# A softmax over 16,384 rows: the first tile loaded in two pieces, and fewer rows scaled on ScalarE

## The chip, the cores and the metric

The kernel runs on one core of one Trainium2 chip. The metric is device time in microseconds (us). The profile's span is about 1.8 us shorter than the time of the same run (160.7 against 162.45 in the kernel before). All runs quoted here were in the same state, called fast, with a granted clock of 1.0 (the share of its full speed that the profile records). The kernel before takes 162.57 us in the median of three runs (162.41 to 162.81). In the batches that follow its median moved between 162.58 and 162.72, so every ratio is taken against the runs of the kernel before in the same session, on the same chip; where two times of different sessions are set side by side, the text says so.

## The reference

```python
def reference(x):                       # x: 16 x 1024 x 512, float32
    x_scaled = x / 0.5
    x_max = np.max(x_scaled, axis=-1, keepdims=True)
    exp_x = np.exp(x_scaled - x_max)
    return exp_x / np.sum(exp_x, axis=-1, keepdims=True)
```

The input is 33.55 MB and so is the output. Each must cross the DMA once: 67.1 MB that no rearrangement of the arithmetic can avoid (the page of the kernel before has 33.55 MB read and 33.55 MB written).

## The kernel before

The 16,384 rows are cut into eight tiles. A tile has 128 partitions with 16 rows of 512 numbers on each (4 MB). The kernel keeps six tiles on the chip at once, so load 6 waits until store 0 has landed, and load 7 waits for store 1 (in the trace the stores land at 69.6 and 89.0 us, and the loads are issued at 69.7 and 89.1). Each tile is worked in blocks of rows: VectorE finds the negated maximum and doubles it (`shift`), ScalarE takes the exponentials row by row and sums them, VectorE inverts the sums, and then VectorE and ScalarE share the scaling.

```python
G = 16                                            # rows per partition and tile
WHOLE = [(0, G)]
LOADS = [[(0, 1), (1, 4), (4, G)]] + [WHOLE] * 7
BLOCKS = [[(0, 4), (4, 8), (8, G)]] + [WHOLE] * 6 + [[(0, 8), (8, G)]]
STORES = [WHOLE] * 8
# ... (cut)
def scale_vector(i):
    c, lo, hi = blocks[i]
    b = hi - lo
    k = b - b // 4                                # VectorE's rows of the block
    # ... reciprocal of the sums (cut)
    rows = chunks[c][:, lo : lo + k, :]
    nc.vector.tensor_mul(
        rows, rows, recips[i][:, 0:k].unsqueeze(2).broadcast_to((P, k, D)))

def scale_scalar(i):                              # ScalarE's rows of the block
    c, lo, hi = blocks[i]
    b = hi - lo
    for g in range(b - b // 4, b):
        row = chunks[c][:, lo + g, :]
        nc.scalar.activation(out=row, in_=row, func=COPY, scale=recips[i][:, g : g + 1])
# ... (cut)
shift(0); shift(1); exponentials(0)
for i in range(n):                                # n = 11 blocks
    if i + 1 < n: exponentials(i + 1)
    scale_vector(i)
    scale_scalar(i)
    if i + 2 < n: shift(i + 2)
    store(i)                                      # issued by ScalarE when the tile is complete
```

Of the kernel before, what the change touches and what calls it, by code (L numbers as in the profile page):

```python
# [1 line left out]

# [4 lines left out]


@with_exitstack
def kernel(  # L10
    ctx: ExitStack,
    tc: tile.TileContext,
    x: bass.AP,
    out: bass.AP,
):
    nc = tc.nc
    fp32 = mybir.dt.float32
    P = nc.NUM_PARTITIONS
    AX = mybir.AxisListType.X
    EXP = mybir.ActivationFunctionType.Exp  # L20
    COPY = mybir.ActivationFunctionType.Copy
    MAX = mybir.AluOpType.max

    D = x.shape[-1]
    xf = x.flatten_outer_dims()
    of = out.flatten_outer_dims()
    N = xf.shape[0]




    G = 16
    C = N // (P * G)
    assert C * P * G == N
    xr = xf.rearrange("(c p g) d -> c p g d", p=P, g=G)
    outr = of.rearrange("(c p g) d -> c p g d", p=P, g=G)
    WHOLE = [(0, G)]
    LOADS = [[(0, 1), (1, 4), (4, G)]] + [WHOLE] * 7
    BLOCKS = [[(0, 4), (4, 8), (8, G)]] + [WHOLE] * 6 + [[(0, 8), (8, G)]]
    STORES = [WHOLE] * 8  # L40
    BMAX = 16
    BUFS = 6

    data = ctx.enter_context(tc.tile_pool(name="data", bufs=BUFS))
    stats = ctx.enter_context(tc.tile_pool(name="stats", bufs=6))

    ctx.enter_context(tc.manual_schedule())


    warm = stats.tile([P, 1], fp32, name="warm", bufs=1)  # L50
    nc.vector.memset(warm, 0.0)  # L51
    nc.scalar.activation(out=warm, in_=warm, func=EXP)  # L52

    chunks = {}
    blocks = [(c, lo, hi) for c in range(C) for lo, hi in BLOCKS[c]]
    n = len(blocks)
    biases, sums, recips = {}, {}, {}

    def load(c):
        if c < BUFS:  # L60
            chunks[c] = data.tile([P, G, D], fp32, name="xt")
        else:
            chunks[c] = chunks[c - BUFS]
        xt = chunks[c]
        for lo, hi in LOADS[c]:
            nc.sync.dma_start(out=xt[:, lo:hi, :], in_=xr[c][:, lo:hi, :])  # L66

    def shift(i):
        c, lo, hi = blocks[i]
        if c not in chunks:  # L70
            load(c)
        b = hi - lo
        negmax = stats.tile([P, BMAX], fp32, name="negmax")
        nc.vector.tensor_reduce(  # L74
            negmax[:, 0:b], chunks[c][:, lo:hi, :], axis=AX, op=MAX, negate=True
        )
        biases[i] = stats.tile([P, BMAX], fp32, name="bias")
        nc.vector.tensor_scalar_mul(biases[i][:, 0:b], negmax[:, 0:b], 2.0)  # L78

    def exponentials(i):  # L80
        c, lo, hi = blocks[i]
        sums[i] = stats.tile([P, BMAX], fp32, name="sums")
        for g in range(hi - lo):
            row = chunks[c][:, lo + g, :]
            nc.scalar.activation(  # L85
                out=row,
                in_=row,
                func=EXP,
                bias=biases[i][:, g : g + 1],
                scale=2.0,  # L90
                accum_out=sums[i][:, g : g + 1],
            )


    def scale_vector(i):
        c, lo, hi = blocks[i]
        b = hi - lo
        k = b - b // 4
        recips[i] = stats.tile([P, BMAX], fp32, name="recip")
        nc.vector.reciprocal(recips[i][:, 0:b], sums[i][:, 0:b])  # L100
        rows = chunks[c][:, lo : lo + k, :]
        nc.vector.tensor_mul(  # L102
            rows, rows, recips[i][:, 0:k].unsqueeze(2).broadcast_to((P, k, D))
        )

    def scale_scalar(i):
        c, lo, hi = blocks[i]
        b = hi - lo
        for g in range(b - b // 4, b):
            row = chunks[c][:, lo + g, :]  # L110
            nc.scalar.activation(  # L111
                out=row, in_=row, func=COPY, scale=recips[i][:, g : g + 1]
            )

    def store(i):
        c, _, end = blocks[i]
        for lo, hi in STORES[c]:
            if hi == end:
                nc.scalar.dma_start(  # L119
                    out=outr[c][:, lo:hi, :], in_=chunks[c][:, lo:hi, :]  # L120
                )

    shift(0)
    shift(1)
    exponentials(0)
    for i in range(n):
        if i + 1 < n:
            exponentials(i + 1)
        scale_vector(i)
        scale_scalar(i)  # L130
        if i + 2 < n:
            shift(i + 2)
        store(i)


# [1 line left out]
_INS = ['x']  # L137
_OUTS = [((16, 1024, 512), 'float32')]


# [23 lines left out]
```

## Time and profile before

| | before |
|---|---|
| time | 162.57 us |
| VectorE (DVE) busy | 125.6 us, 78% of the span |
| ScalarE (ACT) busy | 112.5 us, 70% |
| DMA | 9 tenths or more in all slices but the first and the last |
| last store issued, and landed | 140.3 us, 159.6 us |

The first lines of the page: busy time by engine, then the span in 40 equal slices (each digit is the busy share in tenths), and what the DMA moved in each.

```profile
span 160.7 us, 421 instructions
## 1 busy us (share of the span) xinstructions
DVE 125.6 (78%) x45; ACT 112.5 (70%) x290; POOL 0.2 (0%) x4
## 2 busy tenths in 40 slices
DVE  0507999999999999999999999999799994800000
ACT  3071759089989989995999599959998969600000
...
DMA  5999999999999999999999999999999999999993
```

VectorE and ScalarE stop some 20 us before the end, and the DMA does not. That points to the DMA as the bound; e4 below tests it. How hard the DMA works is in the view by stretches of time (start and end of the stretch in us, its length, busy us of each engine, then the clock, the DMA's share and GB/s):

```profile
5.00:45.00 40.00, 34.23 (x17) 25.24 (x68) 0.00 (x0) 1.00 1.01 434
45.00:90.00 45.00, 44.83 (x11) 41.71 (x109) 0.00 (x0) 1.00 1.01 426
90.00:130.00 40.00, 38.69 (x13) 35.88 (x92) 0.00 (x0) 1.00 1.00 433
...
140.00:156.00 16.00, 0.24 (x1) 0.00 (x0) 0.00 (x0) 1.00 1.00 432
```

The rate is the same 426 to 434 GB/s whether the DMA only loads (first line), loads and stores, or only stores (last line). The trace's record of single packets says the same thing more sharply: 96% of the 32 KB packets hold their DMA engine for 1.213 us, and 16 engines x 32,768 bytes / 1.213 us = 432 GB/s.

The costs that the change touches are in the groups of instructions (line of the code, engine, operation, shapes, count, then total us, mean ns of one, and idle time before them):

```profile
L74 DVE TENSOR_REDUCE negmax<-xt 128x16 f32<-128x8192 f32 x6 | 52.1, 8678 | 0.0
L102 DVE TENSOR_TENSOR xt<-xt,recip 128x6144 f32<-128x6144 f32 x6 | 39.3, 6558 | 0.2
L111 ACT ACTIVATE xt<-xt,recip 128x512 f32<-128x512 f32 x32 | 20.5, 706 | 0.0
L74 DVE TENSOR_REDUCE negmax<-xt 128x8 f32<-128x4096 f32 x3 | 13.2, 4414 | 1.1 <-DMA xt<-in_x_dram 1.1
L102 DVE TENSOR_TENSOR xt<-xt,recip 128x3072 f32<-128x3072 f32 x3 | 10.1, 3358 | 0.1
```

A multiply of 12 rows takes 6558 ns and one of 6 rows 3358 ns, so a row costs (6558 - 3358) / 6 = 533 ns on VectorE in this multiply. And the end of the timeline (start us, duration us, engine, line, operation; in brackets the idle time before it and what ended it):

```profile
136.51 2.55 ACT L111 ACTIVATE xt<-xt,recip 128x512 f32<-128x512 f32 x4
136.65 0.20 DVE L100 RECIPROCAL recip<-sums 128x8 f32<-128x8 f32 x1 [2.32 <-ACT xt L85]
136.88 3.36 DVE L102 TENSOR_TENSOR xt<-xt,recip 128x3072 f32<-128x3072 f32 x1
140.32 0.34 ACTq L119 DMA_DIRECT2D out_dram<-xt  x1
```

The last line is the last store's issue. It lands only 19.2 us later, because nearly the whole of the store before is still ahead of it: in the packet records that one's packets run from 138.93 to 149.54 us, and the last store's own begin at 148.61. That queue is the slack of the arithmetic.

### The profile page before, as it was taken

The page shows a single profiled execution, that of the slowest core. Times are in us where ns is not written, and L with a number is a line of the kernel's source. Part 1 is how long each engine was busy: PE and PEld are TensorE (multiplying, and loading weights), DVE is VectorE, ACT ScalarE, POOL GpSimd, SP SyncE. Part 2 cuts the span into 40 slices and gives each one's busy share as a digit, 9 for nine tenths or more (in the row PEclk, how much of TensorE's full clock was granted, in tenths as well). Part 3 has the DMA queues.
Part 4 walks back from the last instruction along what each step waited for, and adds up shares of the span by engine and source line. Part 5 has one row for each costly group of instructions (what it writes and reads, how often), then busy time and mean ns, then how long its engine had stood idle before and what let it go on. Part 6 is the DMA issues. An engine that isn't in the chain of part 4 may idle for free.

```text
span 160.7 us, 421 instructions
## 1 busy us (share of the span) xinstructions
DVE 125.6 (78%) x45; ACT 112.5 (70%) x290; POOL 0.2 (0%) x4
## 2 busy tenths in 40 slices
DVE  0507999999999999999999999999799994800000
ACT  3071759089989989995999599959998969600000
POOL 0000000000000000000000000000000000000000
DMA  5999999999999999999999999999999999999993
GB/s 169 477 398 465 449 392 465 449 392 443 465 392 392 400 392 498 416 392 473 441 394 457 449 400 441 465 400 432 473 400 416 481 400 416 489 400 408 498 400 139
DMA packets 2595, 67.13 MB, mean 418 GB/s; under 512 B 289, under 2 KB 289, under 8 KB 545
## 3 DMA queue, kind: packets, MB, share of 16 engines
q1 hardware_dynamic: 1440, 33.56, 49.3%
q10 hardware_dynamic: 1152, 33.55, 48.4%
q14 instruction: 3, 0.02, 0.0%
HBM read 33.55 MB, written 33.55 MB: 418 GB/s over the span
## 4 chain that ended last, share of the span: by engine, by line
DMA 41%; DVE 24%; ACT 19%; issue 1%; SPq 1%; ACTq 0%
DMA xt<-in_x_dram 23%; DMA out_dram<-xt 18%; ACT xt L85 17%; DVE negmax L74 15%; DVE xt L102 8%; ACT xt L111 2%; DVE bias L78 1%; SPq L66 1%; DVE recip L100 0%; ACTq L119 0%; ACTq L85 0%
## 5 line engine op out<-in xcount | busy, mean ns | idle before, releaser
L85 ACT ACTIVATE xt<-xt,bias 128x512 f32<-128x512 f32 x128 | 90.4, 707 | 25.8 <-DVE bias L78 24.8
L74 DVE TENSOR_REDUCE negmax<-xt 128x16 f32<-128x8192 f32 (+2 forms) x11 | 69.9, 6353 | 10.7 <-DMA xt<-in_x_dram 10.7
L102 DVE TENSOR_TENSOR xt<-xt,recip 128x6144 f32<-128x6144 f32 (+2 forms) x11 | 52.9, 4813 | 0.4
L85 ACT ACTIVATION_READ_ACCUMULATOR xt<-xt,bias 128x1 f32 x128 | 23.9, 187 | 0.0
L111 ACT ACTIVATE xt<-xt,recip 128x512 f32<-128x512 f32 x32 | 20.5, 706 | 0.0
L100 DVE RECIPROCAL recip<-sums 128x16 f32<-128x16 f32 (+2 forms) x11 | 2.4, 218 | 2.3 <-ACT xt L85 2.3
L78 DVE TENSOR_SCALAR bias<-negmax 128x16 f32<-128x16 f32 (+2 forms) x11 | 1.9, 173 | 0.4
L52 ACT ACT_TABLE_LOAD x1 | 1.3, 1283 | 0.7 <-PEq L148 0.7
L51 DVE MEMSET warm<- 128x1 f32 x1 | 0.1, 59 | 0.8 <-PEq L148 0.8
L52 ACT ACTIVATE warm<-warm 128x1 f32<-128x1 f32 x1 | 0.2, 203 | 0.0
L148 POOL MEMSET const-bfloat16-1.0<- 128x1 bf16 x1 | 0.1, 102 | 0.0
L148 POOL MEMSET const-uint8-127<- 128x1 uint8 x1 | 0.1, 102 | 0.0
L148 POOL MEMSET const-float32-0.0<- 128x1 f32 x1 | 0.1, 99 | 0.2 <-issue 0.2
L148 POOL MEMSET const-float32-1.0<- 128x1 f32 x1 | 0.1, 99 | 0.0
## 6 DMA issues: line engine op xcount, KB each, us to landing
out_dram<-xt ACTq DMA_DIRECT2D x8, 4096.0 KB, 24.8
xt<-in_x_dram SPq DMA_DIRECT2D x7, 4096.0 KB, 29.8
xt<-in_x_dram SPq DMA_DIRECT2D x1, 3072.0 KB, 11.3
xt<-in_x_dram SPq DMA_DIRECT2D x1, 768.0 KB, 4.5
xt<-in_x_dram SPq DMA_DIRECT2D x1, 256.0 KB, 2.8
```

The costliest lines, as they stand in the source:

```text
L51: nc.vector.memset(warm, 0.0)
L52: nc.scalar.activation(out=warm, in_=warm, func=EXP)
L66: nc.sync.dma_start(out=xt[:, lo:hi, :], in_=xr[c][:, lo:hi, :])
L74: nc.vector.tensor_reduce(negmax[:, 0:b], chunks[c][:, lo:hi, :], axis=AX, op=MAX, negate=True)
L78: nc.vector.tensor_scalar_mul(biases[i][:, 0:b], negmax[:, 0:b], 2.0)
L85: nc.scalar.activation(out=row, in_=row, func=EXP, bias=biases[i][:, g : g + 1], scale=2.0, accum_out=sums[i][:, g : g + 1],)
L100: nc.vector.reciprocal(recips[i][:, 0:b], sums[i][:, 0:b])
L102: nc.vector.tensor_mul(rows, rows, recips[i][:, 0:k].unsqueeze(2).broadcast_to((P, k, D)))
L111: nc.scalar.activation(out=row, in_=row, func=COPY, scale=recips[i][:, g : g + 1])
L148: nc = _bacc.Bacc("TRN2", target_bir_lowering=False, num_devices=1)
```

## The change

Two edits in one. There is one DMA fewer at the start (17 in all instead of 18), and less work for ScalarE, which both scales rows and issues the stores. ScalarE scales one row in eight instead of one in four, so 15 rows instead of 32; blocks of four rows are now scaled on VectorE alone.

```diff
-    LOADS = [[(0, 1), (1, 4), (4, G)]] + [WHOLE] * 7
+    LOADS = [[(0, 4), (4, G)]] + [WHOLE] * 7
@@ scale_vector
-        k = b - b // 4
+        k = b - b // 8
@@ scale_scalar
-        for g in range(b - b // 4, b):
+        for g in range(b - b // 8, b):
```

## The prediction

> # Prediction
>
> **What bounds the kernel now: the DMA.** In the slice table its row reads 9 in all slices but the first and last; the stretches table gives about 433 GB/s over every long stretch from 5 to 158 us. The kernel moves 67.13 MB, all compulsory: 155 us at that rate, plus about 2 us before packets flow, 1.4 us from the last bytes to the landing (159.5) and 1.2 us of end. [...]
>
> Compute is shorter: VectorE 125.6 us busy (78%), ScalarE 112.5 (70%). In the timeline the last arithmetic ends at 140.24 us and the last store is issued at 140.32, with one whole store still queued ahead. The chain of waits names VectorE and ScalarE for 43% of the span, but those pieces run under a full DMA.
>
> **What the change does.**
> 1. Loads: one DMA of 1 MB instead of 256 KB + 768 KB; one issue of 0.4 us falls away. Bytes moved by 5 us show that the ramp costs some tenths now: worth 0 to 0.3 us. VectorE's first block waits for both pieces already (starts 5.74).
> 2. ScalarE's scaled rows go from 32 to 15 (blocks of four keep none): 17 x 0.706 = 12 us less, to 100.5.
> 3. VectorE takes those 17 rows. Its multiplies take 6.558, 3.358 and 1.758 us for 12, 6 and 3 rows, so 0.533 us a row: +9.1 us, to 134.7. Its period per tile goes from 15.55 to 16.62 us, still under the DMA's 19.4 (8.39 MB).
>
> **On the critical path.** ScalarE's saving gains nothing directly: VectorE's biases and scaling pace it. VectorE's 9.1 us eat the slack to the DMA's end. VectorE now waits 1.1 us for the last load and 2.3 us for the last sums; about 1.6 us of the addition disappears there. So the last multiply ends at 140.24 + 9.1 - 1.6 = 147.7 us, and the last three stores are issued at about 125.6, 133.3 and 147.8 (4.6, 3.7 and 7.4 us later). In the present trace (158.1 - 147.8) x 433 = 4.5 MB are left at 147.8, against 4.19 MB in the last store: the queue is almost, but just not, empty when it comes. With 1 us from issue to first packet (as at the start) the DMA runs dry for about 0.3 us. That is what the start gains. Loads 6 and 7 wait for the landings of stores 0 and 1, whose issues move by under 1 us.
>
> **Predicted time:** 162.6 us, 8 in 10 between 161.9 and 164.0. Faster by over 2%: 0.02; within 2%: 0.94; slower by over 2%: 0.04. A wash; VectorE is brought to the edge of limiting too.
>
> **What would show it.** Right: VectorE 134 to 135.5 us, ScalarE 100 to 101; last store issued at 147 to 149, landing in 11 to 12 us instead of 19.2; DMA share near 1 up to 156; 17 DMA issues; first reduction at 5 to 5.8 us; VectorE never idle over 0.5 us between 13 and 144; the chain of waits nearly unbroken on VectorE up to the last store. Wrong: a hole in the DMA share at 146 to 150, or VectorE's second reduction starting far from 13.
>
> **What would make it wrong.** Packets of the last store spread unevenly over the 16 engines with no other store beside it (1 to 2 us slower); a VectorE row dearer than 0.533 us; later stores that reorder the loads so that VectorE waits for one; a first megabyte that lands sooner (some tenths faster).

The 162.6 us are the 162.57 of the kernel before with two changes that nearly cancel, 0 to 0.3 us gained at the start and about 0.3 us lost where the DMA was to run dry. The "1 to 2 us slower" for unevenly spread packets was a guess, worked out from no trace.

## The result, and the profile after

The changed kernel takes 162.31 us (median of four runs, 162.22 to 162.53); the kernel before, in the same session, 162.69 (162.41 to 162.97). The ratio is 0.9979, with a 95% interval from 0.9957 to 1.0, which counts as the same (a difference counts from 2%). Here and below, a ratio is the mean time of one kernel's fast runs over that of the other's of the same rounds, so it is not quite the ratio of the medians quoted. Run again later in five rounds (e10, below), the changed kernel's ratio was 0.9988 (0.9974 to 1.0002).

The lines of the page that answer to those of before:

```profile
span 160.6 us, 402 instructions
## 1 busy us (share of the span) xinstructions
DVE 134.6 (84%) x45; ACT 102.1 (64%) x273; POOL 0.2 (0%) x4
## 2 busy tenths in 40 slices
DVE  0507999999999999999999999999999999957000
ACT  3071549069979963998199909991899891790000
...
DMA  5999999999999999999999999999999999999993
```

VectorE's row is now full to the 35th slice, and the DMA's row is unchanged. The groups and the end of the timeline:

```profile
L102 DVE TENSOR_TENSOR xt<-xt,recip 128x7168 f32<-128x7168 f32 x6 | 45.8, 7626 | 0.2
L74 DVE TENSOR_REDUCE negmax<-xt 128x8 f32<-128x4096 f32 x3 | 13.2, 4411 | 0.0
L102 DVE TENSOR_TENSOR xt<-xt,recip 128x3584 f32<-128x3584 f32 x3 | 11.7, 3891 | 0.1
L111 ACT ACTIVATE xt<-xt,recip 128x512 f32<-128x512 f32 x15 | 9.9, 706 | 0.0
```

```profile
143.22 1.32 ACT L111 ACTIVATE xt<-xt,recip 128x512 f32<-128x512 f32 x2
143.35 0.20 DVE L100 RECIPROCAL recip<-sums 128x8 f32<-128x8 f32 x1 [1.79 <-ACT xt L85]
143.59 3.89 DVE L102 TENSOR_TENSOR xt<-xt,recip 128x3584 f32<-128x3584 f32 x1
147.55 0.34 ACTq L119 DMA_DIRECT2D out_dram<-xt  x1
```

Two rows more cost a multiply 7626 - 6558 = 1068 ns, again 534 ns a row. VectorE's wait of 1.1 us for the last load is gone (the second line has 0.0), and the last store is issued 7.2 us later, yet it lands within 0.2 us of the same moment: at 159.7 us, 12.2 us after its issue, against 159.6 us, 19.2 us after its issue. The delay was taken from time that the store spent queueing.

The chain of waits, shares by engine, is where a reader can go wrong. First before, then after:

```profile
DMA 41%; DVE 24%; ACT 19%; issue 1%; SPq 1%; ACTq 0%
```

```profile
DVE 80%; DMA 7%; ACT 4%; issue 0%; SPq 0%
```

Before, the chain ran in part through the DMA; after, it runs almost wholly through VectorE (80%). Read alone, this says that the kernel changed its limit and must have lost or gained. It did neither. The chain follows the last instruction back to what released it. It does not say what the DMA, which ends later still, would have done without it. The two limits now lie about a microsecond apart, by an estimate at the end of the experiments.

### The profile page after: what moved, and what is told of

Same layout as the page of the kernel before. It is cut to its first block, busy times and chain, and to the rows that moved or that the text cites. A ratio compares the mean times of both kernels' runs of the same rounds, so it can differ in the third digit from the quotient of the medians.

```text
span 160.6 us, 402 instructions
## 1 busy us (share of the span) xinstructions
DVE 134.6 (84%) x45; ACT 102.1 (64%) x273; POOL 0.2 (0%) x4
## 4 chain that ended last, share of the span: by engine, by line
DVE 80%; DMA 7%; ACT 4%; issue 0%; SPq 0%
DVE negmax L74 42%; DVE xt L102 36%; DMA xt<-in_x_dram 7%; ACT xt L85 4%; DVE bias L78 1%; DVE recip L100 1%; SPq L66 0%
## 5 line engine op out<-in xcount | busy, mean ns | idle before, releaser
L102 DVE TENSOR_TENSOR xt<-xt,recip 128x7168 f32<-128x7168 f32 (+2 forms) x11 | 62.0, 5637 | 0.4
L111 ACT ACTIVATE xt<-xt,recip 128x512 f32<-128x512 f32 x15 | 9.9, 706 | 0.0
```

The source lines that it names most:

```text
L102: nc.vector.tensor_mul(rows, rows, recips[i][:, 0:k].unsqueeze(2).broadcast_to((P, k, D)))
```

## The experiments

The theory: 67.1 MB through a DMA that is full from 2 to 158 us set the time. The arithmetic costs nothing as long as the last store is issued before the DMA has emptied its queues. Its rivals: the two halves of the change have larger effects that cancel; VectorE sets the time, as the chain says; the DMA alone sets it, whatever the arithmetic does.

### e1: only the loads

```diff
-    LOADS = [[(0, 1), (1, 4), (4, G)]] + [WHOLE] * 7
+    LOADS = [[(0, 4), (4, G)]] + [WHOLE] * 7
```

> The kernel before with the first tile loaded in two pieces (4 and 12 rows) and nothing else changed. My theory (the DMA is full from 2 to 158 us, and only a head start of the DMA counts; the whole gain of the change, about 0.3 us, comes from here): 162.2 to 162.5 us, 0.1 to 0.5 us under before, VectorE 125.6 us busy, last store issued near 140.2. Rival A (the gain comes from relieving ScalarE): no difference from before, within 0.1 us. Rival B (the loads gain a microsecond or more, and VectorE's 9 us pay most of it back): 161.6 us or less.

Measured: 162.5 us (162.3 to 162.65) against 162.64; ratio 0.9989 (0.9974 to 1.0004). VectorE 125.6 us, last store issued at 140.4. The size is as expected, but the interval reaches zero: the head start is not proved.

### e2: only the scaling

```diff
-        k = b - b // 4
+        k = b - b // 8
@@ scale_scalar
-        for g in range(b - b // 4, b):
+        for g in range(b - b // 8, b):
```

> The kernel before with ScalarE scaling one row in eight and the old three loads. My theory: VectorE +9.1 us to 134.7, last store issued near 147.7 instead of 140.3, and the time the same as before within 0.3 us (162.5 to 163.0). Rival A (ScalarE's relief brings the gain): 0.3 us faster than before. Rival B (VectorE's load costs time that the loads pay): 163.3 us or more.

Measured: 162.54 us (162.28 to 163.01) against 162.64; ratio 0.9998 (0.9979 to 1.0016). VectorE 134.6 us, ScalarE 102.1, last store issued at 147.5, landing 12.1 us later. Moving 17 rows costs nothing and gains nothing. The rival with two large effects that cancel falls: neither half alone moves the time by more than 0.3%, by the ends of the intervals.

### e3: all rows on VectorE

Against the changed kernel:

```diff
-        k = b - b // 8
+        k = b - 0
@@ scale_scalar
-        for g in range(b - b // 8, b):
+        for g in range(b - 0, b):
```

> The changed kernel with all rows scaled on VectorE (15 more: +8.0 us). My theory: the slack is used up in the changed kernel; VectorE 142.6 us busy, last store issued near 155.0, landing about 11.8 us later at 166.9, span about 168, time about 169.7 (168.5 to 170.5), DMA share well under 1 between 147 and 156. Rival C (the DMA alone sets the time, the finish of the arithmetic does not matter): 162.3 as before. Rival D (VectorE sets the time in all these kernels, as the chain of waits of the changed one says at 80%): the changed kernel's 9.1 us should have cost something too, and it did not, so this one should also move little.

Measured: 168.74 us (168.71 to 168.81), ratio 1.0374 to the kernel before. VectorE 142.6 us. Both lines, the timeline's last store and the stretches around it, are as the theory says:

```profile
154.98 0.34 ACTq L119 DMA_DIRECT2D out_dram<-xt  x1
```

```profile
140.00:150.00 10.00, 8.91 (x4) 5.55 (x15) 0.00 (x0) 1.00 0.98 419
150.00:154.00 4.00, 3.73 (x2) 0.21 (x2) 0.00 (x0) 1.00 0.00 0
154.00:156.00 2.00, 0.90 (x1) 0.00 (x0) 0.00 (x0) 1.00 0.61 262
156.00:162.00 6.00, 0.00 (x0) 0.00 (x0) 0.00 (x0) 1.00 0.94 404
```

From 150 to 154 us the DMA moves nothing, and after its issue the last store, 4 MB with nothing ahead of it, takes 11.1 us to land. The first 17 rows moved to VectorE cost nothing, and the next 15 (8.0 us of VectorE) cost 6.2 us over e2 of the same session and 6.4 us over the changed kernel's 162.31 of another. So the DMA alone does not set the time, and VectorE alone does not either: in these runs it is whichever ends later. The packet records show a smaller hole before this one: store 6, too, is issued late, at 139.97 us, and from 139.0 to 140.9 us most DMA engines are idle (1.65 us as a mean over the 16; the hole before the last store makes 5.25 us). So in this run a late store 6 left a hole too, and not the last store alone. I was 1 us too high: I had let the store land 11.8 us after its issue instead of 11.1.

### e4: the same DMAs without arithmetic (wrong on purpose)

```diff
-    shift(0)
-    ... (the whole loop)
+    for c in range(C):
+        load(c)
+        nc.scalar.dma_start(out=outr[c], in_=chunks[c])
```

> Wrong on purpose: the same ten loads and eight stores of the kernel before, no arithmetic, each store as soon as its tile has landed. My theory (67.13 MB through a full DMA set the time): 160.5 to 162.8 us, within about 1% of before. Rival D (arithmetic sets the time): clearly less, under 157 us.

Measured: 162.24 us (161.66 to 162.5), ratio 0.9969 (0.9946 to 0.9991); the output is wrong. The softmax kernel is 0.3% (0.1 to 0.5% by the interval) above a bare copy of the same bytes by the same DMAs. This is the strongest single evidence for the theory, and it says how little was left to gain with these DMAs in about this order.

### e5: e3 with the last store in two halves

```diff
-    STORES = [WHOLE] * 8
+    STORES = [WHOLE] * 7 + [[(0, 8), (8, G)]]
```

> The kernel with all rows scaled on VectorE (168.74 us, DMA idle from 150 to 154) with the last tile's store in two halves, each issued when its eight rows are scaled. My theory (there the DMA waits for the last store): the first half is issued at about 150.3 (after the last exponentials on ScalarE), the second at 155.0, and the second half, half as long, lands at about 162; time 164.0 to 165.2 us, 3.5 to 4.7 us less than without the split. Rival (it is slower because VectorE is busier everywhere, not because of the last store): still about 168.7.

Measured: 163.88 us (163.82 to 163.98), ratio 1.0073. The last two stores of its timeline are the halves:

```profile
149.02 0.34 ACTq L119 DMA_DIRECT2D out_dram<-xt  x1
154.95 0.34 ACTq L119 DMA_DIRECT2D out_dram<-xt  x1
```

The second half lands 6.3 us after its issue. With the same VectorE work and the same last multiply as e3, the time falls by 4.9 us (two sessions; the two ratios say the same): e3 was slow chiefly because of what stood behind its last multiply, not because VectorE was busy. The earlier hole, which the split does not touch (139.1 to 140.8 us here, again 1.65 us as a mean over the engines), is large enough for the 1.2 us that e5 still lies above the kernel before. The time came out 0.1 us under my range. The first half was issued 1.3 us earlier than I thought, right after its multiply ended.

### e6: the changed kernel with the last store in two halves

```diff
-    STORES = [WHOLE] * 8
+    STORES = [WHOLE] * 7 + [[(0, 8), (8, G)]]
```

> The changed kernel with the last store in two halves. My theory: the DMA is short of work only for some tenths around 145 in the changed kernel; the first half, issued near 144, fills that, and the time falls by 0 to 0.5 us, to 161.9 to 162.4, no lower than the copy without arithmetic (162.24, 161.66 to 162.5). Rival (the changed kernel is bound by VectorE up to its last store, as its chain of waits says): 158 to 160 us, since half of the last store would no longer follow the last multiply (4.8 us).

Measured: 162.36 us (162.2 to 163.06), ratio 0.9985 (0.9967 to 1.0003). Its halves are issued 3.6 us apart:

```profile
143.85 0.34 ACTq L119 DMA_DIRECT2D out_dram<-xt  x1
147.45 0.34 ACTq L119 DMA_DIRECT2D out_dram<-xt  x1
```

The same edit that is worth 4.9 us in e3 is worth nothing clear of the scatter here. So the changed kernel does not wait for its last multiply, although its chain of waits is 80% VectorE.

### e7 and e8: the first tile in one load

One edit, made in the kernel before (e7) and in the changed kernel (e8):

```diff
-    LOADS = [[(0, 4), (4, G)]] + [WHOLE] * 7        (in e7: the three pieces)
+    LOADS = [WHOLE] * 8
```

> The kernel before (one row in four on ScalarE) with the first tile loaded in one piece. VectorE can start only at 12.9 instead of 5.7 us; its chain moves by about 2.9 us, of which 1.1 is taken up by the wait for the last load: last store issued near 142.1 instead of 140.3. My theory (some 7 us of slack): time as before or a few tenths less, 162.2 to 162.7. Rival (a compute chain from the first load sets the time): 164 us or more.

> The changed kernel (one row in eight on ScalarE) with the first tile loaded in one piece: the same 2.9 us delay of VectorE's start, now with no slack left. My theory: last store issued near 150.5, landing 11 to 12 us later, time 164.3 to 165.4 (1.2 to 1.9% over before), while the same edit costs the kernel before nothing. Rival (DMA alone sets the time): 162.3 in both. Rival (one piece is simply better or worse for the DMA): the same difference in both.

Measured: e7 163.46 us (163.13 to 163.66), ratio 1.0047 (1.0032 to 1.0062); e8 164.44 us (164.37 to 164.51), ratio 1.0108 (1.0092 to 1.0123).

e8 is as expected: last store issued at 150.7, landing 11.1 us later, the landing time of a store with nothing ahead of it. The slack is used up there. e7 is a miss. Its last store is issued at 143.0, so VectorE had time to spare (and the store lands 18.1 us after its issue, behind others), but the kernel still lost 0.8 us where I expected none. So the two kernels differ by 1.0 us under this edit and not by 2. A late last store does not look like e7's cause. The trace's packet records show something else: between 60 and 100 us, packets of 32 KB are longer than 1.213 us by a total of 1.01 us per DMA engine (single ones up to 2.5 us), where in the kernel before this total is 0.02 us. The long ones stand between 75.7 and 88.8 us, after load 6 is issued at 72.43 us (timeline of e7, queue of SyncE):

```profile
72.43 17.52 SPq L66 DMA_DIRECT2D xt<-in_x_dram  x2
```

By then the last packet of load 5 had ended, at 70.62 us (load 4 had landed at 52.2, so the text of e9 below, which has both done at about 71.8, misread the landing of store 0 as a load's): the loads' queue had run empty, and the first packet of load 6 starts only at 76.68. In the kernel before, load 6 is issued at 69.67 us, while packets of load 5 run until 73.96, and its own begin at 74.79. In the meantime the DMA is never idle in e7 (its share is 0.98 from 70 to 80 us, at 410 GB/s): the stores have it to themselves.

e8 has the same empty queue and long packets (0.87 us per engine), but they do not add to its time. After its first load, for which it waits 12.0 us, VectorE waits for no load, so its last store is issued when its own work ends; from 149.4 to 151.6 us most DMA engines are idle, waiting for that store, 1.8 us as a mean over the 16, against the 1.7 us that the kernel lost.

### e9: e7 with the first tile's store in three pieces

```diff
-    STORES = [WHOLE] * 8
+    STORES = [[(0, 4), (4, 8), (8, G)]] + [WHOLE] * 7
```

> Run e7 (one first load, one row in four) came out 0.8 us slower than I expected. In its trace the loads' queue was empty at 72 us: loads 4 and 5 were done at about 71.8, the next load could be issued only at 72.4, when store 0 had landed, and in the 15 us after that 32 KB packets took up to 2.5 us instead of 1.21, worth 1.0 us per DMA engine between 60 and 100 us (0.02 in the kernel before). This kernel is e7 with the first tile's store in three pieces, issued as its 4, 4 and 8 rows are ready, so that store 0 lands some 7 us sooner and the next load is issued while loads are still queued. Theory (empty queue, slow restart): 162.2 to 162.8 us, under 0.2 us of lengthened packets between 60 and 100 us. Rival (the late start of VectorE or the one large load itself costs the 0.8 us): still 163.2 to 163.7.

Measured: 162.75 us (162.56 to 163.18), ratio 1.0009 (0.9992 to 1.0027). Store 0 now starts early, in small parts, and load 6 is issued at 66.85 us:

```profile
66.85 19.72 SPq L66 DMA_DIRECT2D xt<-in_x_dram  x2
```

The packet records, worked out from the four traces:

```
between 60 and 100 us          before    e7      e8      e9
load 6 issued at (us)           69.67   72.43   72.77   66.85
load 5's last packet ends       73.96   70.62   70.22   76.56
load 6's first packet starts    74.79   76.68   77.06   76.93
packets' excess over 1.213      0.02    1.01    0.87    0.02   us per DMA engine
ratio of the time               1       1.0047  1.0108  1.0009
```

VectorE starts as late as in e7 (its first reduction at 12.99 us, in e7 at 12.99), and the first load is as large (4 MB), so neither of these was the cause. The loss goes away (1.0009 instead of 1.0047) in the run whose queue of loads does not run empty. The edit also cuts store 0 into smaller DMAs and brings loads and stores into another order, and no run separates that from the empty queue; that e7 and e8 have the gap and the long packets, and the kernel before and e9 neither, speaks for the queue. In the kernel before, long packets come with the start of the other queue, too: they amount to 0.89 us per engine between 46 and 51 us, after the first store is issued at 45.23 us beside the running loads. What happens inside the DMA when a queue starts beside a busy one is not shown, only that packets were longer in these stretches.

### e10: the changed kernel again

No edit.

> The changed kernel once more, beside the same runs of before, to see whether its 0.2% (0.9979, interval 0.9957 to 1.0) is there. Theory: 162.2 to 162.5, 0.1 to 0.4 us under before; if it is nothing but scatter, within 0.1 us of before.

Measured: 162.46 us (162.28 to 162.59) against 162.58 (162.4 to 163.2); ratio 0.9988 (0.9974 to 1.0002). The gain, if there is one, is about 0.1 to 0.2%, and two sets of runs do not separate it from nothing. This stays open.

### e11: one row in two on ScalarE

In the kernel before:

```diff
-        k = b - b // 4
+        k = b - b // 2
@@ scale_scalar
-        for g in range(b - b // 4, b):
+        for g in range(b - b // 2, b):
```

> The kernel before with ScalarE scaling one row in two (64 rows instead of 32; 4-, 8- and 16-row blocks give 2, 4 and 8). My theory: a share of rows costs nothing as long as the last store is issued before about 148 us; here ScalarE becomes the late one, 112.5 + 32 x 0.61 = 132 us busy, last store issued near 152 to 153, time 166 to 168. Rival (the DMA alone sets the time): 162.6. Rival (VectorE's busy time sets it; here it falls by 17 us): under 162.

Measured: 165.45 us (165.16 to 165.59), ratio 1.0174 (1.0154 to 1.0195); ScalarE 132.1 us, VectorE 109.4. The last store is issued at 151.4, about 1 us before my guess, and the time is half a microsecond under my range; it again lands 11.1 us after its issue. As in e3, the packet records show smaller holes before earlier stores (0.7 and 1.3 us at 130 and 140 us, and 1.3 us before the last one). The valley has two walls: with too many rows on ScalarE (e11, last store issued at 151.4 us) or on VectorE (e3, 155.0) the last store comes after the moment when the DMA runs dry; the hole before it is 1.3 us in e11 and 5.25 us in e3.

One table holds the runs with arithmetic whose last store is whole. The third column is the time from the last store's issue to its landing; its least value is 11.1 us for 4 MB (e3, e8, e11). (The times are of several sessions.)

| run | last store issued | to landing | time (median) |
|---|---|---|---|
| before | 140.3 | 19.2 | 162.57 |
| e1 loads only | 140.4 | 19.2 | 162.50 |
| e2 scaling only | 147.5 | 12.1 | 162.54 |
| the changed kernel | 147.6 | 12.2 | 162.31 |
| e10 the changed kernel again | 147.6 | 12.2 | 162.46 |
| e7 | 143.0 | 18.1 | 163.46 |
| e9 | 143.2 | 17.1 | 162.75 |
| e8 | 150.7 | 11.1 | 164.44 |
| e11 | 151.4 | 11.1 | 165.45 |
| e3 | 155.0 | 11.1 | 168.74 |

All but e7 fit one rule; e7's last store is issued in time, and its loss went with the empty queue of loads. When the DMA stayed full, everything had landed at about 159.6 us (before; 159.7 in the changed kernel); 159.6 - 11.1 = 148.5 us is the latest issue of the last store that costs nothing (an estimate from these numbers; no run has its last store between 147.6 and 150.7). The change moved the issue to 147.6, about 1 us short of it. No version tried beats both kernels beyond the scatter, and the bare copy suggests that about 0.3% is to be had with these DMAs.

## Why the prediction was right or wrong

The prediction held: 162.6 us forecast, 162.31 measured (162.46 when run again), well inside the range, and the same within 2%.

- **The bound.** "What bounds the kernel now: the DMA" is confirmed by e4: a bare copy takes 162.24 us.
- **VectorE.** Forecast +9.1 us to 134.7, measured 134.6. The row price of 0.533 us was exact (0.534).
- **ScalarE.** Forecast 100.5, measured 102.1. This step was mis-sized: I took 17 x 0.706 us, the duration of one row. Rows that follow each other overlap here: four take 2.55 us in the timeline, so each further row adds (2.55 - 0.706) / 3 = 0.61 us, and 17 x 0.61 = 10.4 us is what ScalarE lost. This was off the critical path and did not touch the time.
- **The last three stores.** Forecast at 125.6, 133.3 and 147.8, measured at 125.5, 133.1 and 147.55. The last one "landing in 11 to 12 us": 12.2, a little over, since the queue was not quite empty.
- **The DMA runs dry for about 0.3 us.** It did not. In the changed kernel's packet records 16.0 packets are in flight, one per DMA engine, in every stretch of 3 us from 144 to 156 us. The rate in short stretches dips around 145 us (328 GB/s from 144 to 146), but so it does in e1, whose last store is issued 7 us earlier (295 GB/s in the same stretch). The view books a packet where it starts: in the kernel before it shows 0 GB/s from 159 to 160 us, while the last packets end at 159.22. With packets of 1.213 us, a stretch of 2 us catches one start or two of each engine. A dip in such a short stretch is no hole. This is also the term that was off: I let the data end at 158.1 us, where that view falls off, and so took 4.5 MB to be left at 147.8 us. Up to 159.2 us it would have been about 4.9 MB, and store 6 did keep the engines busy until 149.6 us, 1.2 us after the last store's first packet at 148.4.
- **VectorE's waits.** I wrote that VectorE is never idle over 0.5 us between 13 and 144 us. It is, once: 1.79 us before the last reciprocal. My own sum had left that wait in place; the sentence contradicted it.
- **The gain at the start,** "worth 0 to 0.3 us": e1's difference of 0.1 us and the changed kernel's 0.1 to 0.4 fit it, but none is clear of the scatter.

## What to carry to other kernels

In this kernel, bound by the DMA, arithmetic was free up to a date and costly after it: the first 17 rows moved to VectorE (9.0 us of it) cost nothing that the runs could show (e2, ratio 0.9998), the next 15 (8.0 us) cost 6.2 us (e3). In another kernel of this kind, look for such a date: the time at which a full DMA lands its last byte, minus the time in which the last store lands when nothing is queued ahead of it. Judge a change by what it does to the last store's issue against that date (and look for a hole before an earlier store, as in e3), not by busy shares or by which engine the chain of waits names; and keep a queue of loads from running empty in the middle, because a queue of loads that ran empty and started again beside a busy queue of stores went with a loss of 0.6 to 0.8 us here (e7 against e9 and against the kernel before) with the DMA never idle.
